# Eight cache buffers, packed query blocks, a new stream order and a PSUM copy for the last norm

## The chip, the cores and the metric

The kernel runs on one core of a Trainium2 chip. Time is device microseconds (us) of one execution. A core has TensorE (PE in the rows, its weight loads PEld), VectorE (DVE), ScalarE (ACT), GpSimd (POOL) and SyncE (SP), which here only issues transfers. SBUF holds data and weights, PSUM is where matmuls land.

## The reference, cut to what matters

One step of a one-layer decoder over 256 prompt tokens and 8 sequences of 8 new tokens (T = 320 columns), in float32. Two attention branches read the same normed input: branch 0 picks blocks of 256 keys and takes a softmax, branch 1 is stick-breaking.

```
h = rms_norm(x, g_mix);  qa, ka, va, qs, ks, vs, ga, gs = split(h @ w_in)
o_a = moba_block(rope(qa), cached + new keys and values)      # 8 heads of 64
o_s = stick_breaking_block(qs, cached + new keys and values)  # 8 heads of 64
x  = x + (sigmoid(ga) * (o_a @ w_branch_moba) + sigmoid(gs) * (o_s @ w_branch_sb)) @ w_out
x  = x + (silu(h2 @ w_gate) * (h2 @ w_up)) @ w_down           # h2 = rms_norm(x, g_ffn)
y  = rms_norm(x, g_final)
```

The cache of each sequence is 8 pages of 128 rows, found by a page table; keys and values of both branches together are 64 tiles of 1 MiB.

## The kernel before, in words

Activations lie transposed, features on the 128 partitions and the 320 tokens in columns. A float32 weight tile of 512 KiB is loaded raw (`load_weights`, three raw buffers `wr`) and split into a high part `wh` (an ACT copy, L152) and a rest `wl` (a DVE subtraction, L153), in three pairs of buffers; each dense product is three matmuls of 320 columns (L185, L344), 24 for one tile of output. A raw buffer is free for the next load when its `wl` is written, and a pair when PE has used it.

The first part of the program, up to about half of the span, interleaves six streams. The string `ORDER` (L52) has one letter for each step, and `Plan.run` takes them in that order; the letters set the order on PE, POOL and SP, while DVE and ACT are ordered by a scheduler when the kernel is built. Names for steps in this text:

- **d**: dense work: d1 to d8 queries and keys of branch 0, d9 to d14 its values, d15 to d22 queries and keys of branch 1, then its values and the first branch projection; **g1** to **g16**: the gates.
- **s**: scores of new queries against cached keys (L571), for a pair of sequences in two halves: S1a, S1b, S2a, S2b, S3a and so on. Each half needs two key tiles.
- **a**: three steps for each pair: T1 transposes the weights of pair 1, V1a and V1b multiply them with cached values (L691), two value tiles each; then T2, V2a, V2b. **e**: the end of a pair. **p**: the prompt's own attention.

Cache tiles, keys and values alike, go through one ring of `RB` buffers (`craw`); a buffer is free when the step that reads its tile is done. After each step `Loads.feed` starts at most one cache tile and as many weight tiles as fit. `FIRST` gives the loads begun ahead of the steps: w a weight tile, c a cache tile. Weights and keys go through SP's queue, in program order: if one load has to wait for its buffer, all behind it wait. Values go through POOL's queue as indirect transfers (L541), each behind a copy of one element (L540, `seen`) of the key tile begun next to last, so a value load starts only when that key tile has landed.

The scores multiply a block of 32 query columns, which is PE's stationary side, with 512 key columns; the blocks stand in two tiles `QS` (L592). `rsqrt` (L250) forms the first norm from `sq`, a sum of squares, with six tiny matmuls `cs` (L261) that stand on PE between d3 and d4. At the end `last_norm` (L838) makes the row r in SBUF on DVE, and seven multiplications (L854) form the output, six of 320 columns on DVE and one of 640 on POOL; each is followed by its store, by turns from SP and ACT.

Of the kernel before, what the change touches and what calls it, by code (L numbers as in the profile page):

```python
# [6 lines left out]
F32 = mybir.dt.float32  # L7
F32R = mybir.dt.float32r
I32 = mybir.dt.int32
AF = mybir.ActivationFunctionType  # L10
ALU = mybir.AluOpType
# [3 lines left out]
P = 128  # L15
# [16 lines left out]
SCALE = 0.125  # L32

SB, TB, OB, DB = 2, 3, 1, 2
RB = 7

LAG = 2
PACE = 1
FIRST = "wcwwwcwc"
ORDERED = {mybir.EngineType.PE, mybir.EngineType.Pool, mybir.EngineType.SP}  # L40
STARTED = ORDERED | {mybir.EngineType.DVE, mybir.EngineType.Activation}
WR, WB = 3, 3
# [7 lines left out]


ORDER = (  # L52
    "dddddddsddddsddsaddpsaadasegdsdaaapeddsadpsggdaappeaapdddssp"
    "gpepdgddpsagasapggegapaapgpsseggpggpdsagdasaaedgaaded"
)


# [82 lines left out]
class Net:  # L140
# [60 lines left out]
    def constants2(self):  # L201
        nc, I, c = self.nc, self.I, self.cpool
        self.ident = c.tile([P, P], F32, name="ident")
        self.ones = c.tile([P, P], F32, name="ones")
        self.warm = c.tile([P, 1], F32, name="warm")
        self.seen = c.tile([1, 1], F32, name="seen")
        self.keys = []
        turn = self.fpool.tile([P, HP, T], F32, name="turn", tag="F5", bufs=FB)
        self.cosr, self.sinr = turn[:, 0], turn[:, 1]
        self.rstd = c.tile([P, T], F32, name="rstd")  # L210
        self.rtok = c.tile([P, 3], F32, name="rtok")
        self.diag = c.tile([P, P], F32, name="diag")
        self.small = c.tile([P, NSMALL + NINT], F32, name="small")
        self.g_mix, self.g_ffn, self.g_fin = (self.small[:, 8 * i:8 * i + 8] for i in range(3))
        self.own_mask = [self.small[:, 24 + OWN * i:24 + OWN * (i + 1)] for i in range(2)]
        self.order = self.small[:, 24 + 2 * OWN:24 + 2 * OWN + 4]
        self.eps = self.small[:, 24 + 2 * OWN + 4:24 + 2 * OWN + 5]
        ints = self.small[:, NSMALL:].bitcast(I32)
        nk = DEC_B * N_PAGES
        self.pidx = ints[:, 0:2]  # L220
        self.idx_k = ints[:, 2:2 + nk]
        self.idx_v = ints[:, 2 + nk:].rearrange("p (h b) -> p h b", h=2)
        nc.vector.memset(self.ones, 1.0)

        self.keep_warm(WARM)

    def keep_warm(self, n):

        warm = self.pp.tile([P, 512], F32, name=self.uid("warm"), tag="t", bufs=TB)
        for _ in range(n):  # L230
            self.nc.tensor.matmul(warm, self.ones, self.ones[:, 0:1].to_broadcast([P, 512]), start=True, stop=True)

    def constants3(self):
        nc, I = self.nc, self.I
# [311 lines left out]
    def gen_scores(self, br, u, box):  # L546

        nc, w = self.nc, self.work
        for half in range(2):
            yield (f"qk{br}{int(br or half)}3",), f"s{br}{u}" if half else None  # L550
            raw = [self.loads.take("c") for x in range(2)]
            if half == 0:
                QS = self.made.pop((br, u), None) or self.queries(br, u)
                box["S"] = []
                p = box["p"] = w.tile([P, 8, N_PAGES, 16], F32, name=self.uid("p"), tag="p", bufs=1)
                if br == 0:
                    st = box["st"] = w.tile([P, 32], F32, name=self.uid("st"), tag="st", bufs=2)
                else:
                    s = box["s"] = w.tile([P, NCOL], F32, name=self.uid("s"), tag="s0", bufs=1)
                    kp = box["kp"] = w.tile([P, NCOL + 1], F32, name=self.uid("kp"), tag="s2", bufs=1)  # L560

                    zo = self.own_scores(br, u, QS)
                    nc.vector.memset(kp[:, 0:1], 1.0)
                    nc.scalar.activation(kp[:, 1:1 + OWN], zo, AF.Sigmoid, scale=-SCALE)
                    nc.scalar.activation(s[:, :OWN], zo, AF.Sigmoid, scale=SCALE)
            S = self.pp.tile([P, 512], F32, name=self.uid("S"), tag="s", bufs=SB)
            box["S"].append(S)
            for i in range(2):
                for y in range(4):
                    x, hp, r = y // 2, 2 * (y % 2) + i, slice(32 * y, 32 * y + 32)  # L570
                    nc.tensor.matmul(S[r], QS[:, hp, r], raw[x][:, :, hp * P:(hp + 1) * P], start=i == 0, stop=i == 1)  # L571
            if br == 0:
                Sb = S.rearrange("p (b k) -> p b k", b=2)
                nc.vector.tensor_reduce(st[:, 2 * half:2 * half + 2], Sb, AX.X, ALU.add)
                nc.vector.tensor_reduce(st[:, 15 + 2 * half:17 + 2 * half], Sb, AX.X, ALU.max)
            else:
                c0, c1 = OWN + 512 * half, OWN + 512 * (half + 1)
                nc.scalar.activation(kp[:, c0 + 1:c1 + 1], S, AF.Sigmoid, scale=-SCALE)
                nc.scalar.activation(s[:, c0:c1], S, AF.Sigmoid, scale=SCALE)
                f0 = c0 if half else 0  # L580
                n = c1 - f0 - half
                nc.vector.tensor_tensor_scan(kp[:, f0 + 1:f0 + 1 + n], kp[:, f0 + 1:f0 + 1 + n], self.zeros.to_broadcast([P, n]),
                                             initial=kp[:, f0:f0 + 1], op0=ALU.mult, op1=ALU.add)
                a, d = (v[:, c0:c1].rearrange("p (g j q) -> p j g q", g=4, j=8) for v in (s, kp))
                nc.vector.tensor_mul(p[:, :, 4 * half:4 * half + 4], a, d)
        if br == 0:
            box["zo"] = self.own_scores(br, u, QS)
        later = divmod(HP * br + u + 2, HP)
        if later[0] == br or f"qk{later[0]}03" in self.plan.done:
            self.queries(*later)  # L590

    def queries(self, br, u):  # L592

        nc, t, QS = self.nc, self.B[br], self.QS[u % 2]
        qbase = QS.rearrange("p a b -> p (a b)")
        for e in range(2):
            r = slice(HD * e, HD * e + HD)
            src = t["q"][r, :, NP_ + 16 * u:NP_ + 16 * u + 16].rearrange("p h (x q) -> p h x q", x=2)
            c = qbase[r, 8 * e:8 * e + 8]
            dst = bass.AP(tensor=c.tensor, offset=c.offset, ap=[list(c.ap[0]), [P + 16, HP], [64, 2], [1, 8]])  # L600
            if e:
                nc.scalar.activation(dst, src, AF.Copy)
            else:
                nc.vector.tensor_copy(dst, src)
        self.made[br, u] = QS
        return QS

    def own_scores(self, br, u, QS):
        nc = self.nc
        own = self.pp.tile([P, 512], F32, name=self.uid("own"), tag="t", bufs=TB)  # L610
        for i in range(2):
            for y in range(4):
                x, hp, r = y // 2, 2 * (y % 2) + i, slice(32 * y, 32 * y + 32)
                c = NP_ + 16 * u + 8 * x
                nc.tensor.matmul(own[r, :OWN], QS[:, hp, r], self.B[br]["k"][:, hp, c:c + OWN], start=i == 0, stop=i == 1)
        zo = self.work.tile([P, OWN], F32, name=self.uid("zo"), tag="zo", bufs=2)
        nc.vector.tensor_tensor(zo, own[:, :OWN], self.own_mask[br], ALU.add)
        return zo
# [219 lines left out]
    def last_norm(self, acc, xg):  # L838

        nc, y, x1 = self.nc, self.stg, self.x1  # L840
        ps = self.pp.tile([P, T], F32, name="rb", tag="o", bufs=OB)
        nc.tensor.matmul(ps, self.ones, acc[:, 0], start=True, stop=False)
        for c in (slice(0, T // 2), slice(T // 2, T)):
            nc.tensor.matmul(ps[:, c], self.ones, acc[:, 1, c], start=False, stop=c.stop == T)
        r, w = [y.tile([P, T], F32, name=n, tag="y", bufs=3) for n in ("r", "w")]
        nc.scalar.activation(r, ps, AF.Abs_reciprocal_sqrt, scale=1.0 / D)
        nc.vector.tensor_mul(w, r, r)
        nc.vector.scalar_tensor_tensor(w, w, -0.5 / D, ps, op0=ALU.mult, op1=ALU.mult)
        nc.vector.scalar_tensor_tensor(r, w, 1.5, r, op0=ALU.add, op1=ALU.mult)
        e = 0  # L850
        for i, n in enumerate((1, 1, 1, 1, 1, 1, 2)):
            s = slice(e, e + n)
            engine = nc.gpsimd if i == 6 else nc.vector
            engine.tensor_tensor(x1[:, s], xg[:, s], r[:, None, :].to_broadcast([P, n, T]), ALU.mult)  # L854
            (nc.scalar if i % 2 else nc.sync).dma_start(self.O["y"][:, s], x1[:, s])
            e += n

# [23 lines left out]
    def build(self):  # L881
# [38 lines left out]
        with ExitStack() as top:  # L920
# [8 lines left out]
            with ExitStack() as mid:  # L929
# [7 lines left out]
                self.constants3()  # L937
                self.loads.begin(FIRST[2:])
                self.work = mid.enter_context(pool("work"))
                self.QS = [self.work.tile([P, HP, P], F32, name=f"QS{i}") for i in range(2)]  # L940
                self.zeros = self.work.tile([P, 1], F32, name="zeros")
                for t in (*self.QS, self.zeros):
                    nc.vector.memset(t, 0.0)
# [99 lines left out]
```

## Time and profile before

| | |
|---|---|
| median of 3 runs | 565.85 us (564.5 to 568.01) |
| profiled execution, its own time | 564.84 us |
| its span, first to last instruction | 563.0 us |
| mean granted clock of TensorE | 0.986 of full speed |
| PE, DVE, ACT, POOL busy | 96%, 59%, 48%, 9% |
| read from HBM | 134.22 MB |

How to read the rows below. A row of a timeline has its start in the span, its length, the engine, the line, output and inputs, the count, and in brackets how long the engine stood idle before it and what ended that. The chain of waits is followed back from the last instruction. PE's matmuls overlap each other: a matmul of 320 columns is listed with 0.31 us, but 24 of them follow each other in 3.52 us, so lengths of work are taken from groups in the chain. A window gives the busy time of each engine in a stretch, the granted clock, the share of the 16 DMA engines and the rate in GB/s.

### The profile page before, as it was taken

What the parts mean: (1) busy time and instruction counts of PE and PEld (TensorE: products, weight loads), DVE (VectorE), ACT (ScalarE), POOL (GpSimd) and SP (SyncE); (2) the same over time, 40 slices, a digit from 0 to 9 for tenths busy, and PEclk for the clock granted to TensorE, in tenths of its full rate; (3) what the DMA queues carried; (4) which work ended last, traced back from release to release, by engine and by line L of the source; (5) the groups of instructions that cost most, each with busy time, mean ns of one, the idle gap of its engine ahead of it and who ended that gap; (6) DMA issues with size and microseconds to landing.
All of it is one profiled execution on the core that took longest, in us unless ns stands there. A gap on an engine that the chain in (4) does not pass through costs nothing.

```text
span 563.0 us, 10934 instructions
## 1 busy us (share of the span) xinstructions
PE 543.2 (96%) x4252; PEld 494.0 (88%) x4252; DVE 332.7 (59%) x600; ACT 268.7 (48%) x483; POOL 48.8 (9%) x73
## 2 busy tenths in 40 slices
PE   8899999799999999999999999999999999999992
PEld 6888867578778787977999999999999999999992
DVE  6777675255575746764688656666666665444434
ACT  7775555325675444643446454444444443354321
POOL 0002102140021402131000000000000000000001
PEclk9899999799999999999999999999999999999997
DMA  8899999999699999987595544444444444544512
GB/s 306 296 374 331 368 358 405 413 392 400 225 363 357 352 401 351 383 316 293 198 325 162 150 130 151 146 150 154 149 146 152 150 152 140 153 141 144 161 33 93
DMA packets 45571, 138.86 MB, mean 247 GB/s; under 512 B 5200, under 2 KB 7504, under 8 KB 41296
## 3 DMA queue, kind: packets, MB, share of 16 engines
q1 hardware_dynamic: 40336, 104.06, 54.4%
q0 software_dynamic: 4608, 33.56, 15.0%
q8 instruction: 33, 0.54, 0.4%
q10 hardware_dynamic: 576, 0.56, 0.3%
q14 instruction: 18, 0.15, 0.1%
HBM read 134.22 MB, written 3.93 MB: 245 GB/s over the span
## 4 chain that ended last, share of the span: by engine, by line
PE 81%; DMA 7%; ACT 5%; DVE 3%; SPq 2%; issue 1%; DVEq 0%; POOL 0%; ACTq 0%
PE dps L185 55%; PE dps L344 12%; PE S L571 4%; PE po L691 4%; DMA vr<-in_cv,small 3%; DMA wr<-in_w_in 2%; ACT rot L363 2%; DMA kr<-in_ck 1%; PE dps L388 1%; PE tp L667 1%; PE dps L518 1%; PE tp L504 1%; ACT wh L152 1%; PE dps L463 1%; DVE wl L153 1%
## 5 line engine op out<-in xcount | busy, mean ns | idle before, releaser
L152 ACT ACTIVATE wh<-wr 128x1024 fp32r<-128x1024 f32 (+1 forms) x122 | 127.0, 1045 | 187.0 <-issue 110.9
L153 DVE TENSOR_TENSOR wl<-wr,wh 128x1024 fp32r<-128x1024 f32 (+1 forms) x122 | 146.8, 1205 | 76.9 <-ACT wh L152 76.7
L185 PE MATMUL dps<-x1h,wh 128*128 128x320 f32 x352 | 109.0, 310 | 0.0
L185 PE MATMUL dps<-x1l,wh 128*128 128x320 f32 x352 | 108.8, 309 | 0.0
L185 PE MATMUL dps<-x1h,wl 128*128 128x320 f32 x352 | 108.8, 309 | 0.0
L344 PE MATMUL dps<-xs,wh 128*128 128x320 f32 x256 | 78.5, 319 | 1.6 <-ACT wh L152 1.4
L344 PE MATMUL dps<-xl,wh 128*128 128x320 f32 x256 | 77.2, 314 | 0.2 <-DVE xl L307 0.2
L185 PEld LDWEIGHTS dps<-x1h,wh 128*128 128x128 f32 x352 | 66.1, 188 | 0.1
L185 PEld LDWEIGHTS dps<-x1l,wh 128*128 128x128 f32 x352 | 66.1, 188 | 0.0
L185 PEld LDWEIGHTS dps<-x1h,wl 128*128 128x128 f32 x352 | 66.1, 188 | 0.0
L185 PE MATMUL dps<-fh,wl 128*128 128x320 f32 x176 | 54.4, 309 | 0.0
L185 PE MATMUL dps<-fh,wh 128*128 128x320 f32 x176 | 54.4, 309 | 0.0
L185 PE MATMUL dps<-fl,wh 128*128 128x320 f32 x176 | 54.4, 309 | 0.0
L344 PEld LDWEIGHTS dps<-xs,wh 128*128 128x128 f32 x256 | 48.7, 190 | 4.7 <-ACT wh L152 1.5
L344 PEld LDWEIGHTS dps<-xl,wh 128*128 128x128 f32 x256 | 48.8, 191 | 0.9 <-DVE xl L307 0.9
L344 PE MATMUL dps<-xs,wl 128*128 128x320 f32 x256 | 43.6, 310 | 0.0
L344 PEld LDWEIGHTS dps<-xs,wl 128*128 128x128 f32 x256 | 39.3, 189 | 0.3 <-DVE wl L312 0.3
L541 POOL DMA_INDIRECT vr<-in_cv,small x32 | 33.3, 1040 | 43.1 <-PE po L691 11.4
L691 PE MATMUL po<-vr,pt 128*32 128x256 f32 x512 | 32.3, 394 | 4.4 <-DMA vr<-in_cv,small 4.4
L185 PEld LDWEIGHTS dps<-fh,wh 128*128 128x128 f32 x176 | 33.0, 188 | 0.0
L185 PEld LDWEIGHTS dps<-fl,wh 128*128 128x128 f32 x176 | 33.0, 188 | 0.0
L185 PEld LDWEIGHTS dps<-fh,wl 128*128 128x128 f32 x176 | 33.0, 188 | 0.0
(203 smaller groups left out, 848.9 us busy)
## 6 DMA issues: line engine op xcount, KB each, us to landing
kr<-in_ck SPq DMA_DIRECT2D x128, 256.0 KB
wr<-in_w_ff SPq DMA_DIRECT2D x44, 512.0 KB
wr<-in_w_in SPq DMA_DIRECT2D x30, 512.0 KB
wr<-in_w_down SPq DMA_DIRECT2D x16, 448.0 KB
wr<-in_w_v SPq DMA_DIRECT2D x8, 512.0 KB
wr<-in_w_b SPq DMA_DIRECT2D x8, 512.0 KB
wr<-in_w_out SPq DMA_DIRECT2D x8, 512.0 KB
wr<-in_w_down SPq DMA_DIRECT2D x8, 512.0 KB
```

The lines of the kernel that those rows point to most:

```text
L152: self.nc.scalar.activation(hi, raw, AF.Copy)
L153: self.nc.vector.tensor_tensor(lo, raw, r32(hi), ALU.subtract)
L185: nc.tensor.matmul(ps, w, x, start=first and i == 0, stop=last and i == len(todo) - 1)
L344: self.nc.tensor.matmul(ps, a, x, start=k + low + i == 0, stop=low == 1 and k + n == KD and i == n - 1)
L363: nc.scalar.activation(rot[32 * q:32 * q + 32], ps[32 * s:32 * s + 32], AF.Copy)
L388: nc.tensor.matmul(ps, self.xs[:, k], w[k][j], start=k + j == 0, stop=k + j == KD)
L463: nc.tensor.matmul(S[e][:, i], q[r, 2 * u + i, half * P:half * P + P], k[r, 2 * u + i, half * P:NP_], start=True, stop=True)
L504: nc.tensor.transpose(tp[:, i * P:(i + 1) * P], src, self.ident)
L518: nc.tensor.matmul(po[r, i, :NP_ if kt else P], t["v"][:, kt, c0:c0 + HD], mv, start=kt == 1, stop=kt == 0)
L541: self.nc.gpsimd.indirect_dma_start(out=raw.rearrange("p a b -> p (a b)"), out_offset=None, in_=self.I[f"cv{br}"], in_offset=bass.Indirect ...
L571: nc.tensor.matmul(S[r], QS[:, hp, r], raw[x][:, :, hp * P:(hp + 1) * P], start=i == 0, stop=i == 1)
L691: nc.tensor.matmul(po[r], PT[j][:, r], v[:, c:c + 256], start=j == 0, stop=j == 8)
```

## The change

- `RB` goes from 7 to 8 cache buffers (8 KiB more of each partition). Room comes from `QS`, two tiles of 320 columns in place of 512 (blocks of 32 columns that overlap where they hold zeros), and from `ones`, one column in place of 128, which matmuls now read broadcast.
- `FIRST` goes from "wcwwwcwc" to "wwwwc": two cache tiles and one weight tile fewer are begun ahead of the steps, and the fourth weight tile comes ahead of the first key tile.
- `ORDER` is new from its 12th letter to its 61st.
- In `last_norm` ACT copies r into a PSUM bank; five of DVE's six output multiplications read that copy.

```diff
-RB = 7
+RB = 8
-FIRST = "wcwwwcwc"
+FIRST = "wwwwc"
-    "dddddddsddddsddsaddpsaadasegdsdaaapeddsadpsggdaappeaapdddssp"
+    "dddddddsdddsdddsdaspaddsadasegaddaapedsapdpsggdaapepaaddgpds"
...
-        self.ones = c.tile([P, P], F32, name="ones")
+        self.ones = c.tile([P, 1], F32, name="ones")
...
-                    nc.tensor.matmul(S[r], QS[:, hp, r], raw[x][:, :, hp * P:(hp + 1) * P], start=i == 0, stop=i == 1)
+                    nc.tensor.matmul(S[r], self.block(QS, x, hp), raw[x][:, :, hp * P:(hp + 1) * P], start=i == 0, stop=i == 1)
...
-            dst = bass.AP(tensor=c.tensor, offset=c.offset, ap=[list(c.ap[0]), [P + 16, HP], [64, 2], [1, 8]])
+            dst = bass.AP(tensor=c.tensor, offset=c.offset, ap=[list(c.ap[0]), [48, HP], [160, 2], [1, 8]])
...
+    def block(self, QS, x, hp):
+
+        c = 48 * hp - 16 * (hp % 2)
+        return QS[:, x, c:c + 32]
...
+        ones = self.ones.to_broadcast([P, P])
+        nc.tensor.matmul(ps, ones, acc[:, 0], start=True, stop=False)
...
+        rb = self.pp.tile([P, T], F32, name="rstd3", tag="s", bufs=SB)
+        nc.scalar.activation(rb, r, AF.Copy)
...
-            engine = nc.gpsimd if i == 6 else nc.vector
-            engine.tensor_tensor(x1[:, s], xg[:, s], r[:, None, :].to_broadcast([P, n, T]), ALU.mult)
+            engine, v = (nc.gpsimd, r) if i == 6 else (nc.vector, rb if i else r)
+            engine.tensor_tensor(x1[:, s], xg[:, s], v[:, None, :].to_broadcast([P, n, T]), ALU.mult)
...
-                self.QS = [self.work.tile([P, HP, P], F32, name=f"QS{i}") for i in range(2)]
+                self.QS = [self.work.tile([P, 2, 160], F32, name=f"QS{i}") for i in range(2)]
```

Three places show what the change moves. The first is DVE near the start, around d3 (`wl_164` and `wl_152` are the rest of d3's weights, `wl_259` that of d4's, `sq` is what `cs` reads):

```order
-L153 TENSOR_TENSOR wl_164<-wr_122,wh_163 128x1024
+L153 TENSOR_TENSOR wl_152<-wr_122,wh_151 128x1024
 L319 TENSOR_TENSOR sq_106<-sq_106 128x1280
+L153 TENSOR_TENSOR wl_259<-wr_124,wh_258 128x1024
 L319 TENSOR_TENSOR sq_106<-sq_106 128x640
 L321 TENSOR_TENSOR sq<-sq_106 128x320
```

The weights of d4 are now split between the first and the last two additions of `sq`. Before, they were split behind them, as ACT copied their high part only behind eight copies `rot`; on ACT that copy has moved ahead of the eight.

The second place is SP's queue where the keys of S3a (`kr_889` before, `kr_768` now) are begun. Before:

```order
L157 DMA wr_656<-in_w_in 128x1024
L157 DMA wr_692<-in_w_in 128x1024
L157 DMA wr_694<-in_w_in 128x1024
L157 DMA wr_825<-in_w_in 128x1024
L157 DMA wr_827<-in_w_in 128x1024
L529 TENSOR_LOAD small
L533 ISA
L533 DMA kr_889<-in_ck 128x512
```

and now:

```order
L157 DMA wr_601<-in_w_in 128x1024
L157 DMA wr_659<-in_w_in 128x1024
L157 DMA wr_695<-in_w_in 128x1024
L157 DMA wr_697<-in_w_in 128x1024
L529 TENSOR_LOAD small
L533 ISA
L533 DMA kr_768<-in_ck 128x512
```

The weights of d18 and d19 (`wr_825`, `wr_827`) stood ahead of these keys and now stand behind them; what stands ahead are those of d15, d16, d17 and g1. On PE, V2a and V2b stood together behind d18; now V2a stands ahead of d18, and V2b behind d19.

The third place is the end of DVE's program; the seventh row of the multiplications is POOL's and unchanged:

```order
-L849 SCALAR_TENSOR_TENSOR r<-w,r 128x320
-L854 TENSOR_TENSOR x_3741<-xg,r 128x320 x6
...
+L855 SCALAR_TENSOR_TENSOR r<-w,r 128x320
+L863 TENSOR_TENSOR x_3741<-xg,r 128x320
+L863 TENSOR_TENSOR x_3741<-xg,rstd_6371 128x320 x5
```

Five of the six now read `rstd`, the copy in PSUM, which ACT writes behind r.

## Rows read from the trace of the kernel before

**Rows 1.** The page: granted TensorE clock in 40 equal slices, in tenths

```profile
PEclk9899999799999999999999999999999999999997
```

**Rows 2.** Who PE waited for: us in total, times, longest

```profile
PE po L691 <- DMA vr<-in_cv,small: 4.4, 2, 3.5
PE dps L344 <- ACT wh L152: 1.4, 1, 1.4
...
PE S L571 <- ACT QS L602: 0.9, 1, 0.9
...
PE dps L185 <- DVE wl L153: 0.5, 1, 0.5
```

**Rows 3.** The chain that ended last, in order of time: start, us, what

```profile
50.72 1.89 PE dps L388 x16
...
66.58 1.23 DVE wl L153
...
88.11 14.16 DMA vr<-in_cv,small
102.31 4.44 PE po L691 x36
...
171.59 3.52 PE dps L344 x24
...
191.03 2.16 PE po L691 x40
...
329.70 221.98 PE dps L185 x1512
...
557.64 1.61 DVE x L854 x4
```

**Rows 4.** Windows: busy time of PE, PEld, DVE, ACT, POOL, then clock, DMA share, GB/s

```profile
0.00:60.00 60.00, 55.47 (x368) 47.84 (x369) 40.98 (x85) 42.16 (x83) 5.21 (x15) 0.97 0.93 332
60.00:90.00 30.00, 30.00 (x284) 22.91 (x286) 19.00 (x48) 16.91 (x44) 6.28 (x9) 1.00 0.97 359
90.00:105.00 15.00, 10.60 (x120) 6.51 (x116) 6.17 (x18) 5.62 (x16) 2.29 (x4) 0.83 1.03 419
...
20.00:25.00 5.00, 4.52 (x20) 4.52 (x21) 4.02 (x8) 2.79 (x5) 0.00 (x0) 0.66 0.59 197
...
100.00:105.00 5.00, 2.69 (x28) 1.31 (x32) 0.00 (x0) 0.00 (x0) 1.88 (x3) 0.50 1.06 420
```

**Rows 5.** Timelines of ACT, DVE and PE near the start, and PE at V2a

```profile
15.84 3.51 ACT L363 ACTIVATE rot<-dps 32x320 f32<-32x320 f32 x8
...
31.55 1.06 ACT L152 ACTIVATE wh<-wr 128x1024 fp32r<-128x1024 f32 x1 [2.95 <-DMA wr<-in_w_in]
...
17.72 0.49 DVE L321 TENSOR_TENSOR sq<-sq 128x320 f32<-128x320 f32 x1
...
18.27 0.83 PE L261 MATMUL cs<-ones,sq 128*128 128x1 f32 x6 [0.29 <-DVE sq L321]
...
95.36 1.93 PE L691 MATMUL po<-vr,pt 128*32 128x256 f32 x32
```

**Rows 6.** Timeline of SP's queue at the keys of S3a; value tiles, issue to landing

```profile
50.63 17.53 SPq L157 DMA_DIRECT2D wr<-in_w_in  x5
69.33 1.93 SPq L533 DMA_DIRECT2D kr<-in_ck  x4
...
DMA to landing us min/median/max: 6.3/9.7/14.2
```

**Rows 7.** Timelines of DVE and POOL: two instructions that overlap

```profile
237.14 0.49 DVE L438 TENSOR_TENSOR y<-dps,rstd 128x320 f32<-128x320 f32 x1 [0.98 <-PE dps L344]
...
237.34 0.18 POOL L540 COPY seen<-kr 1x1 f32<-1x1 f32 x1
```

**Rows 8.** The output multiplications L854: duration in ns min/median/max; POOL's row

```profile
L854 DVE TENSOR_TENSOR x<-xg,r x6: 478/480/1817, 555.4 to 558.8; 128x320 f32<-128x320 f32 x6
...
555.70 1.60 POOL L854 TENSOR_TENSOR x<-xg,r 128x640 f32<-128x640 f32 x1 [299.98 <-DVE r L849]
```

More of the change, by code (lines that the diff above doesn't have):

```diff
@@ L52 @@
 ORDER = (
-    "dddddddsddddsddsaddpsaadasegdsdaaapeddsadpsggdaappeaapdddssp"
-    "gpepdgddpsagasapggegapaapgpsseggpggpdsagdasaaedgaaded"
+    "dddddddsdddsdddsdaspaddsadasegaddaapedsapdpsggdaapepaaddgpds"
+    "spepdgddpsagasapggegapaapgpsseggpggpdsagdasaaedgaaded"
 )
@@ L230, in keep_warm @@
         for _ in range(n):
-            self.nc.tensor.matmul(warm, self.ones, self.ones[:, 0:1].to_broadcast([P, 512]), start=True, stop=True)
+            self.nc.tensor.matmul(warm, self.ones.to_broadcast([P, P]), self.ones.to_broadcast([P, 512]), start=True, stop=True)
     def constants3(self):
@@ L614, in own_scores @@
                 c = NP_ + 16 * u + 8 * x
-                nc.tensor.matmul(own[r, :OWN], QS[:, hp, r], self.B[br]["k"][:, hp, c:c + OWN], start=i == 0, stop=i == 1)
+                nc.tensor.matmul(own[r, :OWN], self.block(QS, x, hp), self.B[br]["k"][:, hp, c:c + OWN], start=i == 0, stop=i == 1)
         zo = self.work.tile([P, OWN], F32, name=self.uid("zo"), tag="zo", bufs=2)
@@ L841, in last_norm @@
         ps = self.pp.tile([P, T], F32, name="rb", tag="o", bufs=OB)
-        nc.tensor.matmul(ps, self.ones, acc[:, 0], start=True, stop=False)
+        ones = self.ones.to_broadcast([P, P])
+        nc.tensor.matmul(ps, ones, acc[:, 0], start=True, stop=False)
         for c in (slice(0, T // 2), slice(T // 2, T)):
-            nc.tensor.matmul(ps[:, c], self.ones, acc[:, 1, c], start=False, stop=c.stop == T)
+            nc.tensor.matmul(ps[:, c], ones, acc[:, 1, c], start=False, stop=c.stop == T)
         r, w = [y.tile([P, T], F32, name=n, tag="y", bufs=3) for n in ("r", "w")]
```

## The prediction

> **What bounds the kernel now.** I read the granted clock first, then PE's waits, then the chain, then windows of the stretches where something waits. From 272 us on the chain is PE alone, one stretch of 222 us among it [rows 3]. The change leaves that work and its order as they are, so it can move the time in three places only: the start, the six streams up to 272 us, and the end behind the last matmul. Up to 272 us PE waits little: 4.4 us in two waits of V2b for its second pair of value tiles, and 1.4, 0.9 and 0.5 us near the start [rows 2]. To these come stretches at half clock (1.2 in place of 2.4 GHz), which show as slices below 9 [rows 1]: the windows 20 to 25 and 100 to 105 us have 0.66 and 0.50 [rows 4]. Both follow a gap on PE.
>
> What made V2b wait is a transfer. Its last value tile was begun at 88.11 and took 14.16 us [rows 3], the longest of the value tiles, whose median is 9.7 [rows 6]. In 90 to 105 us the DMA engines moved 419 GB/s at a share of 1.03, so they were full; in 60 to 90 us it was 359 GB/s, and in 0 to 60 us 332 [rows 4]. So the tile was late because less was moved earlier, not for want of engines at the end. One reason stands in SP's queue: five weight loads took it from 50.63 for 17.53 us, since each waits until a raw buffer has been split, and the keys of S3a behind them began only at 69.33 [rows 6].
>
> **Term 1, the wait of V2b.** It costs 4.4 us of idle [rows 2] and a slow stretch: 36 matmuls took 4.44 us where 40 take 2.16, that is 1.94 for 36, so 2.50 more [rows 3]. Together 6.9 us.
>
> Three edits meet here. The order puts V2a ahead of d18 and V2b behind d19. A dense step is 3.52 us [rows 3], so V2a, at 95.36 [rows 5], comes 3.5 earlier and V2b as much later; with the 0.9 us of term 2, V2a starts at about 90.9. The weights of d18 and d19 no longer hold up the keys of S3a. The last of the four weight loads still ahead of them waits for a split that follows the end of d11. That ends at 50.72 + 1.89 = 52.61 before [rows 3], now about 1 us later, since S1b, about 2 us by the value steps' row, goes ahead of it and 0.9 us are gained. The ACT copy (1.06, [rows 5]) and the DVE rest (1.23, [rows 3]) bring it to 56. So these keys begin at 56 to 58 in place of 69.33. And the eighth buffer lets each cache tile begin one tile earlier where buffers were what it waited for.
>
> What V2a needs by 90.9 is, in the order of the loads, 18 cache tiles of 1.05 MB, 20 weight tiles of 0.52 MB and 1.8 MB of inputs and constants: 31.2 MB, and with some 1 MB of later tiles that share the engines 32.2. By 60 us 332 x 60 = 19.9 MB were there [rows 4]; I take the same for after: its queue starts poorer, with two cache tiles fewer begun, but the hole at 20 to 25 us, 197 GB/s [rows 4], closes, as the raw buffer of d4's weights is split sooner. The other 12.3 MB take 29.4 us at 419 GB/s and 34.3 at 359 [rows 4]. So they are there between 89.4 and 94.3. I take the rate between, 389: 91.6, a wait of 0.7. V2b then has two dense steps, 7 us, more for its two tiles, and I expect no wait there. For what I cannot see I make the rest 1.2 us: a gain of 6.9 - 1.2 = 5.7. The bounds are 6.9, and 0.5 where the rate stays at 359: then V2a waits 3.4 to 3.9 and the slow stretch comes too, 6.4 in all.
>
> **Term 2, the start.** Between d3 and d4 PE waits for `cs` 0.29 us, runs it from 18.27 [rows 5], and waits 1.4 for d4's weights [rows 2], because ACT made eight `rot` copies first, 3.51 us from 15.84 [rows 5]. Now the weights' copy goes ahead of the eight, so d4 needn't wait. But on DVE their rest, 1.23 us [rows 3], goes ahead of the last additions of `sq`, which ended at 18.21 [rows 5]; so `cs` comes 1.2 us later, and the wait only moves: a gain of 0.2. The gap stays about as long, so I leave the slow stretch behind it. It would give back some 1.7 us: the clock missing in the window 20 to 25, 0.34 x 5 us [rows 4]. Later S1a waits 0.9 for the query blocks, which ACT copies behind three groups of `rot`, and d9 0.5 for weights [rows 2]. ACT had stood 2.95 us for the weight tile ahead of these groups [rows 5]; with no key tile in front of it that tile comes sooner, but one more weight copy of 1.06 us now stands ahead of the query blocks. I take half of the 1.4: 0.7. Term 2 is 0.9, between -1.1 (the copy has no cover) and 3.3.
>
> **Term 3, the end.** Of DVE's six multiplications five take 0.48 us and one 1.82, while POOL's runs 1.60 from 555.70 [rows 8]: with both inputs in SBUF the second DVE row ended only behind POOL's. A DVE row with one input in PSUM overlapped a POOL copy at 237.3, and neither was longer than alone [rows 7]. So five rows that read the copy should run through POOL's. DVE's first row, 0.48 from 555.41, covers ACT's copy of r, which by 1.06 us for 1024 columns [rows 5] I put at 0.5 with its hand-over, so the second begins at about 556.0. Rows follow each other every 0.40 (four in 1.61, [rows 3]), so the sixth ends at 558.1 in place of 557.64 + 1.61 = 559.25: 1.15 us. If a long POOL row does block it, unlike the short copy, the gain is 0, and the hand-over makes it -0.5.
>
> **Term 4, what costs.** Steps have new neighbours: S2b comes close behind S2a, the two halves of the prompt's second pair stand almost together, d18 and d19 follow V2a. PE's waits of this kind now are 0.3 to 0.9 us [rows 2, 5]. I charge one, 0.3, between 0 and 1.5. At nothing I cost `ones` as one column and the query blocks: as many instructions of the same size on PE; the fill of the blocks on DVE shrinks and lies ahead of nothing that PE waits for.
>
> **Sum.** 5.7 + 0.9 + 1.15 - 0.3 = 7.45 us. The profiled execution's own time of 564.84 becomes 557.4. It lies 1.0 below the median of the runs, 565.85, from which I take the same: 558.4, 1.3% less.
>
> **Rivals.** The first, the transfers stay the bound: the eighth buffer doesn't raise the rate, because SP stood on splits of weights and not on cache buffers [rows 6]. Then V2a waits as V2b did, term 1 is 0.5, the sum 2.25, and the time 563.6. For it speaks a share of 0.93 and 0.97 already [rows 4]; against it 419 GB/s behind 359, and that the keys of S3a leave the jam. The Trainium skill has a rule for it (DMA: Bandwidth & Descriptors, "Where 436 GB/s comes from"): between HBM and SBUF the memory's side binds at about 358 GB/s for a core. By it the rate of 60 to 90 us was the ceiling and the time would be this rival's 563.6. The 419 GB/s over 15 us differ from it, so I give this rival no more than its other reasons earn.
>
> The second, the start's slow stretch goes with its cause: if `cs` comes less late than I think, PE stays at full clock, and 1.7 us more are gained: 556.7. Against it: the moved wait is as long as the old.
>
> The third, slower. The value tiles of V1b are now held by `seen` until the keys of S3a have landed, where before an earlier key tile sufficed. PE reaches V1b at about 78: from there to V2a, 90.9, stand V1b itself with 2.2 us, d17 with 3.5, T2 with 1, S3b with 2, and e1 and g1 with 3.7 [rows 3]. If these keys still began at 69.33, as before [rows 6], I put their landing 4 us behind their last issue, at 75; the second value tile, 1.3 later, lands 9.7 to 14.2 after that [rows 6], at 86 to 90, a wait of 8 to 12 us with a slow stretch of 2.5. That alone is some 12.5; the tiles of V2 come late by as much and the 5.7 of term 1 are lost: 565.85 + 12.5 - 1.75 = 576.6. It decides from keys that begin later than 62 (78 less 9.7, 1.3 and 5). I have them at 56.
>
> **How the numbers follow.** The forecast gets 0.60, the first rival 0.24, the second 0.10, the third 0.06. About 1% (5.7 us) is what a measurement can tell from no change: faster means under 560.2. The forecast falls beyond that with 0.07 of its 0.60 (a wait of 3 us or more at V2a), and all but a sixth of the second rival lies under it: faster 0.61; the first rival and the 0.07 make same 0.33; slower 0.06. The range takes in the first rival and goes down to where terms 1 to 3 are near their best (6.9 + 3.3 + 1.3 = 11.5): 554.5 to 564.5.
>
> **What would show it.** Term 1: PE's waits for value tiles in 60 to 110 us under 2 us in sum, no clock below 0.9 there, the rate of 60 to 90 us above 380 GB/s, the keys of S3a begun by 60. Term 2: `cs` starts at about 19.5 and d4 right behind it. Term 3: no multiplication over 0.6 us on DVE. Wrong would be a wait as long as the old at V2a or V1b, a new wait of PE behind 110 us where the same bytes are now wanted some 7 us earlier, or a row of 1.8 us at the end.

## The result and the profile after

The changed kernel takes 559.05 us (median of 4 runs, 557.76 to 559.79) beside 566.31 us for the kernel before (median of 4): ratio 0.987, interval 0.9833 to 0.9907. Run again beside the experiments it took 558.35 us, ratio 0.9865 (0.9843 to 0.9886). The forecast was 558.4 us and faster by over 1%: both hold. The sum behind it holds less well, as its terms show.

The granted clock of the profiled execution (span 558.0 us), to be read against [rows 1], then who PE waited for, against [rows 2] (us in total, times, longest):

```profile
PEclk9899999999999999999999999999999999999998
```

```profile
PE po L696 <- DMA vr<-in_cv,small: 2.9, 3, 1.3
PE cs L261 <- DVE sq L321: 1.3, 1, 1.3
```

The low slice at 98 to 112 us (the 7) is gone, the one at 14 to 28 us is there. The wait for value tiles (L691 is L696 now) is 2.9 us in place of 4.4, and no piece is longer than 1.3. Windows of the same stretches as [rows 4] (busy PE, PEld, DVE, ACT, POOL, then clock, DMA share, GB/s):

```profile
0.00:60.00 60.00, 56.40 (x382) 47.94 (x386) 40.75 (x87) 43.85 (x87) 3.67 (x12) 0.97 0.94 343
60.00:90.00 30.00, 29.38 (x292) 21.46 (x285) 19.66 (x50) 13.07 (x33) 7.81 (x12) 1.00 0.99 364
90.00:105.00 15.00, 13.67 (x134) 11.02 (x132) 6.34 (x16) 7.99 (x19) 2.29 (x4) 1.00 1.02 413
20.00:25.00 5.00, 4.70 (x23) 4.70 (x24) 3.78 (x13) 3.51 (x6) 0.00 (x0) 0.66 1.04 361
100.00:105.00 5.00, 5.00 (x61) 3.96 (x59) 2.88 (x5) 1.31 (x2) 0.00 (x0) 1.00 1.03 415
```

The rates are a little higher up to 90 us (343 and 364 for 332 and 359), and there is no half clock at 100 us. PE at the two value steps that still wait, V1b (from 77.86) and V2a (from 91.91):

```profile
77.86 0.60 PE L696 MATMUL po<-vr,pt 128*32 128x256 f32 x4
79.08 1.71 PE L696 MATMUL po<-vr,pt 128*32 128x256 f32 x26 [0.62 <-DMA vr<-in_cv,small]
...
91.91 0.63 PE L696 MATMUL po<-vr,pt 128*32 128x256 f32 x4
93.86 1.92 PE L696 MATMUL po<-vr,pt 128*32 128x256 f32 x28 [1.33 <-DMA vr<-in_cv,small]
```

SP's queue around the keys of S3a (the eight `kr`), and POOL's around V1b's two value tiles:

```profile
46.22 10.73 SPq L157 DMA_DIRECT2D wr<-in_w_in  x4
58.12 5.04 SPq L533 DMA_DIRECT2D kr<-in_ck  x8
```

```profile
64.90 0.18 POOL L540 COPY seen<-kr 1x1 f32<-1x1 f32 x1 [13.24 <-DMA kr<-in_ck]
65.73 1.90 POOL L541 DMA_INDIRECT vr<-in_cv,small  x1 [0.65 <-DMA kr<-in_ck]
67.64 0.18 POOL L540 COPY seen<-kr 1x1 f32<-1x1 f32 x1
67.98 0.97 POOL L541 DMA_INDIRECT vr<-in_cv,small  x1 [0.16 <-issue]
```

The keys begin at 58.12 in place of 69.33 [rows 6]. But `seen` holds V1b's value tiles until 64.90; the second begins at 67.98 and PE goes on at 79.08, 11.1 us later, where it had been ready before. V2a's two value tiles are held in the same way, until 81.18, and the second is begun at 83.23:

```profile
81.18 0.18 POOL L540 COPY seen<-kr 1x1 f32<-1x1 f32 x1 [12.24 <-DMA kr<-in_ck]
...
83.23 0.97 POOL L541 DMA_INDIRECT vr<-in_cv,small  x1 [0.16 <-issue]
```

The end of the program, DVE and then POOL:

```profile
551.38 0.49 DVE L863 TENSOR_TENSOR x<-xg,r 128x320 f32<-128x320 f32 x1
551.86 2.08 DVE L863 TENSOR_TENSOR x<-xg,rstd 128x320 f32<-128x320 f32 x5
```

```profile
551.66 1.60 POOL L863 TENSOR_TENSOR x<-xg,r 128x640 f32<-128x640 f32 x1 [302.18 <-DVE r L855]
```

The five rows that read the copy in PSUM run through POOL's row in 2.08 us; none stalls as the one of 1.82 did [rows 8].

**Where the time went, by places of equal work.** Between fixed points of PE's program the lengths mostly repeat to 0.1 us from run to run wherever PE doesn't wait, so a stretch that is longer has a wait or a slow clock in it. The points are the starts of S2a, of S4a and of the last stretch of 1512 matmuls (329.70 before, [rows 3]), and the end of the span. S2a and S4a before, then S2a, S4a and the last stretch in the changed kernel:

```profile
60.37 1.92 PE L571 MATMUL S<-kr,QS 128*32 128x512 f32 x16
115.87 1.92 PE L571 MATMUL S<-kr,QS 128*32 128x512 f32 x16
```

```profile
59.06 1.92 PE L571 MATMUL S<-kr,QS 128*32 128x512 f32 x16
110.91 1.49 PE L571 MATMUL S<-kr,QS 128*32 128x512 f32 x12
325.67 221.97 PE dps L185 x1512
```

Medians belong to the runs, the other columns to one profiled execution each. The profile of the row "changed, again" is called the second profile below; the rows under it are the experiments of the next section.

| kernel | to S2a | S2a to S4a | to last stretch | to the end | median us | ratio to before, interval |
|---|---|---|---|---|---|---|
| before | 60.37 | 55.50 | 213.83 | 233.30 | 566.31 | |
| changed | 59.06 | 51.85 | 214.76 | 232.33 | 559.05 | 0.987 (0.9833 to 0.9907) |
| changed, again | 57.94 | 51.34 | 215.07 | 232.35 | 558.35 | 0.9865 (0.9843 to 0.9886) |
| e1_seven | 59.08 | 53.05 | 218.84 | 232.33 | 563.84 | 0.9943 (0.9909 to 0.9977) |
| e2_oldstream | 66.42 | 56.70 | 213.97 | 232.31 | 568.41 | 1.0041 (1.0024 to 1.0059) |
| e5_firstold | 64.54 | 48.65 | 214.30 | 232.31 | 561.09 | 0.9902 (0.9867 to 0.9936) |
| e13_oldorder | 58.10 | 55.57 | 214.47 | 232.36 | 561.66 | 0.9902 (0.987 to 0.9934) |
| e10_packonly | 62.10 | 56.03 | 214.48 | 233.59 | 570.34 | 1.0083 (1.0049 to 1.0118) |
| e7_gate | 58.38 | 49.83 | 213.32 | 232.37 | 555.5 | 0.981 (0.9785 to 0.9835) |
| e7_again | 58.30 | 50.49 | 214.21 | 232.30 | 557.34 | 0.9848 (0.9809 to 0.9888) |
| e9_gate2 | 57.98 | 51.30 | 213.73 | 232.39 | 557.59 | 0.9861 (0.9841 to 0.9882) |
| e12_gate1 | 57.54 | 53.32 | 215.93 | 232.31 | 560.27 | 0.9892 (0.9849 to 0.9935) |
| e3_oldtail | 57.88 | 51.53 | 214.76 | 233.63 | 558.91 | 0.9882 (0.9858 to 0.9905) |
| e4_tailsbuf | 58.81 | 51.55 | 214.63 | 233.61 | 559.47 | 0.9881 (0.9855 to 0.9908) |

The experiments ran in three groups, each on one chip with the kernel before beside them (medians 565.94, 565.97 and 566.64 us); the first group is e1, e2, e5 and e7_gate, the second the changed kernel again, e3, e4 and e9, the third the rest. Four rows (changed, changed again, e3, e4) are kernels that differ by their edits at the end alone. Among them the first column scatters by 1.2 us, the second by 0.5 and the third by 0.4, so smaller differences in a column mean nothing by themselves.

### The profile page after: what moved, and what is told of

Same layout as the page of the kernel before. It is cut to its first block, busy times and chain, and to the rows that moved or that the text cites. A ratio compares the mean times of both kernels' runs of the same rounds, so it can differ in the third digit from the quotient of the medians.

```text
span 558.0 us, 10927 instructions
## 1 busy us (share of the span) xinstructions
PE 542.0 (97%) x4252; PEld 493.2 (88%) x4252; DVE 329.7 (59%) x600; ACT 269.9 (48%) x484; POOL 49.8 (9%) x73
## 4 chain that ended last, share of the span: by engine, by line
PE 82%; DMA 9%; DVE 3%; ACT 2%; SPq 1%; issue 1%; POOL 1%; DVEq 0%; POOLq 0%; ACTq 0%
PE dps L185 55%; PE dps L344 15%; PE po L696 4%; DMA vr<-in_cv,small 4%; DMA kr<-in_ck 3%; PE S L571 3%; DMA wr<-in_w_in 1%; DVE wl L153 1%; SPq L533 1%; PE tp L504 1%; PE tp L672 1%; PE dps L518 1%; PE dps L388 1%; PE dps L463 1%; DMA small<-in_c_small 1%
## 5 line engine op out<-in xcount | busy, mean ns | idle before, releaser
L541 POOL DMA_INDIRECT vr<-in_cv,small x32 | 35.9, 1121 | 19.1 <-PE po L696 8.6
L696 PE MATMUL po<-vr,pt 128*32 128x256 f32 x512 | 32.1, 381 | 2.9 <-DMA vr<-in_cv,small 2.9
```

The source lines that it names most:

```text
L541: self.nc.gpsimd.indirect_dma_start(out=raw.rearrange("p a b -> p (a b)"), out_offset=None, in_=self.I[f"cv{br}"], in_offset=bass.Indirect ...
L696: nc.tensor.matmul(po[r], PT[j][:, r], v[:, c:c + 256], start=j == 0, stop=j == 8)
```

## The experiments

### The parts apart: buffers, order, first loads, packing

The question: which part brings the gain in the middle, S2a to S4a. Each edit is against the changed kernel.

**e1_seven**: one buffer less.

```diff
-RB = 8
+RB = 7
```

> The changed kernel with seven cache buffers in place of eight; all else is as changed. Theory (the order did it: V2b stands a dense step later, the keys of S3a no longer wait behind the weights of d18 and d19): value waits of PE in 60 to 110 us stay under 4 us in sum, no clock below 0.9 there, about 560 to 561 us, some 1 to 2 above the changed kernel. Rival (the eighth buffer did it): the long wait comes back at V1b, V2a or V2b, 4 us or more with a stretch at half clock, 564 to 566 us.

It took 563.84 us, with single runs from 559.48 to 568.46. That is close to the rival's time, but not by the rival's wait: V1b, V2a and V2b wait for no tile, and no half clock follows. The start is as in the changed kernel; the middle is 1.2 to 1.7 us longer, and behind S4a 3.8 to 4.1 more are lost, where the next value step, V3a, waits 2.96 us. In the middle S3a, begun at 76.14, waits for a key tile:

```profile
80.52 1.48 PE L571 MATMUL S<-kr,QS 128*32 128x512 f32 x10 [3.33 <-DMA kr<-in_ck]
```

```profile
60.00:90.00 30.00, 26.67 (x254) 19.55 (x250) 17.01 (x41) 12.87 (x32) 6.89 (x12) 1.00 0.91 338
```

The rate of 60 to 90 us is 338 GB/s where eight buffers have 364 and, in the second profile, 373: the eighth buffer does raise it, and with this order it is worth 4 to 5.5 us, most of it later than the prediction looked.

**e2_oldstream**: eight buffers, packing and the new end, with the order and first loads of before.

```diff
-FIRST = "wwwwc"
+FIRST = "wcwwwcwc"
-    "dddddddsdddsdddsdaspaddsadasegaddaapedsapdpsggdaapepaaddgpds"
-    "spepdgddpsagasapggegapaapgpsseggpggpdsagdasaaedgaaded"
+    "dddddddsddddsddsaddpsaadasegdsdaaapeddsadpsggdaappeaapdddssp"
+    "gpepdgddpsagasapggegapaapgpsseggpggpdsagdasaaedgaaded"
```

> Eight buffers, packed query blocks and the PSUM copy at the end, but ORDER and FIRST of before. Theory (the order did it): V2b still waits about 4 us and the clock falls behind it; what is left of the gain is the end, 1.3 us, and little more: 564 to 565 us. Rival (the eighth buffer did it): the wait at V2b is under 1.5 us, no half clock there, 559 to 561 us.

It is slower than before, 568.41, and both expectations missed. I read its SP queue first, where six weight loads stood for 24.95 us ahead of S3a's keys, and took the old order for the cause. The table says otherwise: against the kernel before, 6.05 us are lost ahead of S2a and 1.2 in the middle (this profiled execution is 2.8 us over its kernel's median). Most of the loss at the start is a wait for weights with a slow stretch behind it:

```profile
48.22 0.38 PE L185 MATMUL dps<-wh,xs 128*128 128x256 f32 x1 [1.56 <-ACT wh L152]
49.48 0.58 PE L185 MATMUL dps<-wl,xs 128*128 128x256 f32 x1 [0.88 <-DVE wl L153]
49.86 0.41 PE L185 MATMUL dps<-wh,xl 128*128 128x256 f32 x1
50.08 0.41 PE L185 MATMUL dps<-wh,xs 128*128 128x256 f32 x1
```

Rows of 0.28 us at full clock are 0.41 here, and they follow each other every 0.21 us in place of 0.12; the granted clock of 50 to 55 us is 0.50.

**e5_firstold**: the old first loads alone, **e13_oldorder**: the old order alone; each takes its one edit from the diff of e2.

> The changed kernel with FIRST of before (wcwwwcwc): the first key tile goes into the queue ahead of the fourth weight tile. Theory (bytes bound V1b and V2a): the DMA share of 10 to 15 us goes from 0.43 to about 1.0, so 1 MB more is moved early, the waits at V1b and V2a (1.9 us as listed) shrink by 1 to 2 us; at the start the 1.3 us wait ahead of cs turns back into a wait of 1.4 us ahead of d4: 557 to 558.5 us. Rival (these waits come from the gate and from the queue's order): they stay within 0.5 us, time within 1 us of the changed kernel.

> The changed kernel with the order of the kernel before, but the new first loads (in the run e2_oldstream both were old: 568.4). It parts the two. Theory: the old order is what hurts, since five to six weight loads stand ahead of S3a's keys, and the first loads only cost at the start: 565 to 567, keys of S3a not begun before 68, a value wait of 3 us or more. Rival: the old first loads made that jam, since two more cache tiles taken at the start leave the queue poorer; then 560 to 562.

Between e13 and e2 only the first loads differ: 58.10 against 66.42 us up to S2a. So the time that I had expected of e13 was wrong and its rival's was right: 561.66. The jam in SP's queue is there all the same, as is a wait of V2b for a value tile, so in the middle nothing is gained:

```profile
46.68 19.41 SPq L157 DMA_DIRECT2D wr<-in_w_in  x5
67.26 4.96 SPq L533 DMA_DIRECT2D kr<-in_ck  x8
```

```profile
100.59 3.20 PE L696 MATMUL po<-vr,pt 128*32 128x256 f32 x26 [3.50 <-DMA vr<-in_cv,small]
```

Between e13 and the changed kernel only the order differs: 55.57 against 51.85 and 51.34. This is what the new order brings with eight buffers, 3.7 to 4.2 us. e5 took 561.09 us, above both expectations: the waits at V1b and V2a went, as its theory said, but the start lost more than they gave. It comes to S2a 5.5 to 6.6 us later, and then waits for no value tile between S2a and S4a, 48.65 us. A late PE gives the transfers time; so about half of what is lost at the start comes back.

**e10_packonly**: the kernel before with the packed query blocks and the one column of ones, and nothing else of the change.

```diff
-        self.ones = c.tile([P, P], F32, name="ones")
+        self.ones = c.tile([P, 1], F32, name="ones")
...
-                    nc.tensor.matmul(S[r], QS[:, hp, r], raw[x][:, :, hp * P:(hp + 1) * P], start=i == 0, stop=i == 1)
+                    nc.tensor.matmul(S[r], self.block(QS, x, hp), raw[x][:, :, hp * P:(hp + 1) * P], start=i == 0, stop=i == 1)
```

> The kernel before with the packed query blocks and ones as one column alone: seven buffers, the old order, the old first loads and the old end. The prediction costed these two edits at nothing. Theory: the time of the kernel before within 1 us, 565 to 567, and its wait at V2b. Rival: a smaller stationary tile that lies closer together, or ones read with a step of zero, costs or gives back something on each of these matmuls; then the time differs by more than 1.5 us and the score steps (1.74 us from S to V) are longer or shorter.

It is 3.7 us slower than the kernel before beside it (570.34 for 566.64), so "at nothing" was wrong, and not by way of the matmuls that read the blocks: S2b to V1a is 1.9 us in both (69.8 to 71.7 and 71.6 to 73.5). DVE and ACT are ordered by the scheduler when the kernel is built, and here it made another order; which of the two edits led it there, the smaller fills or the column of ones, no run tells. ACT's instructions between the queries of S1 and the first values, before and then e10 (`wh_583` and `wh_649` are weights, `rot_641` reads what PE makes in the step ahead):

```
L152 ACTIVATE wh_544<-wr_367 128x1024
L152 ACTIVATE wh_583<-wr_456 128x1024
L363 ACTIVATE rot_641<-dps_616 32x320 x4
L383 ACTIVATE v_234<-dps_658,rtok 128x256
L152 ACTIVATE wh_649<-wr_509 128x1024
```

```
L152 ACTIVATE wh_544<-wr_367 128x1024
L363 ACTIVATE rot_641<-dps_616 32x320 x4
L152 ACTIVATE wh_583<-wr_456 128x1024
L152 ACTIVATE wh_649<-wr_509 128x1024
L383 ACTIVATE v_234<-dps_658,rtok 128x256
```

In the trace of e10 the `rot` waits for PE, the copy of `wh_583` behind it ends at 46.73, and PE, which needs it, stands:

```profile
41.63 1.06 ACT L152 ACTIVATE wh<-wr 128x1024 fp32r<-128x1024 f32 x1
43.89 1.75 ACT L363 ACTIVATE rot<-dps 32x320 f32<-32x320 f32 x4 [1.20 <-PE dps L344]
45.67 1.06 ACT L152 ACTIVATE wh<-wr 128x1024 fp32r<-128x1024 f32 x1
```

```profile
46.78 0.39 PE L185 MATMUL dps<-wh,xs 128*128 128x256 f32 x1 [0.87 <-ACT wh L152]
48.04 0.39 PE L185 MATMUL dps<-wl,xs 128*128 128x256 f32 x1 [0.87 <-DVE wl L153]
```

In this execution, the quickest of the seven of e10, the span is 3.2 us longer than before's; 2.0 of them lie between S1a and S2a, where these waits are (24.13 us for 22.09), and the granted clock stays at 1.00 behind them; in e2 it falls to 0.50 from 50 to 55 us behind 1.56 and 0.88 us. The other runs of e10 have a lower mean clock (0.976 to 0.990 for 0.991), so a slow stretch may make up the rest of the 3.7; no trace of theirs shows where.

The same two waits stand in e2 and e5, the other kernels with packed blocks and the old first loads, and in no kernel with the new ones. With the packing the new first loads are worth 6.7 us in the old order (e2 to e13, medians on two chips) and 2.0 to 2.7 in the new one (e5 to the changed kernel). What they are worth without the packing is not known, since no run has them alone. In the trace of before, which has neither, this cost and its cure can't be seen.

### What held V1b

The question: is it the gate `seen` that delays V1b, or are the engines too full to bring its tiles sooner. Three kernels change which key tile holds the value loads.

**e7_gate**, V1b's two loads wait for the fourth last key tile:

```diff
-            self.nc.gpsimd.tensor_copy(self.seen, self.keys[-LAG][0:1, 3, 511:512])
+            back = 4 if (br, b // 2, half) == (0, 0, 1) else LAG
+            self.nc.gpsimd.tensor_copy(self.seen, self.keys[-back][0:1, 3, 511:512])
```

> The changed kernel, where the two value tiles of V1b follow an older key tile (the fourth from last begun, as before the change) in place of the keys of S3a. Theory (the gate makes V1b wait): they are begun some 3 us sooner, at about 61 to 63 in place of 65.7 and 68.0, and V1b does not wait; 1 to 1.5 us less than the changed kernel. Rival (the engines are full, so what V1b gains V2a or S3a loses): the wait at V1b goes, that at V2a grows by as much, time within 0.5 us.

> The kernel of e7_gate once more, on another chip. Theory: 555.5 again, no loss at V1b, and none at the value step at 184 us. Rival: that run was lucky in when single transfers landed, as the scatter of the changed kernel's waits suggests; then 557 to 559.

**e12_gate1**, the same with `back = 1`: the last key tile.

> The changed kernel with the two value loads of V1b held until the last key tile in the queue has landed, instead of the one before it: the opposite of e7_gate. Theory (the gate sets V1b): these loads begin some 2 to 3 us later, at 66 to 68 us, V1b loses 3 to 4.5 us instead of 1.0 to 1.3, the streams behind it come later by as much, and the time is 561 to 562. Rival (the loads would wait for full engines anyway, and e7_gate won by chance): 558 to 559.

**e9_gate2**, as e7_gate, with V2a's two loads (`(0, 1, 0)`) among those that wait for the fourth last.

> The changed kernel with the two value loads of V1b and the two of V2a held by the landing of the fourth last key tile instead of the second last (in the run e7_gate it was V1b's alone, 555.5). Theory (the gate, not the engines, set when value tiles came): V2a's tiles begin at about 70 instead of 79 to 81, its wait of 0.55 goes, and the time is 0.5 to 1 us under that run, about 554.8. Rival (the engines are full by then): the bytes of V2a's tiles delay the keys of S3b or the weights of d17 and d18, PE waits there by 1 to 3 us, and the time is 556 to 558.

V1b of e7_gate, its second tile begun at 61.88 (POOL, then PE):

```profile
60.58 0.96 POOL L542 DMA_INDIRECT vr<-in_cv,small  x1 [9.57 <-DMA kr<-in_ck]
61.55 0.18 POOL L541 COPY seen<-kr 1x1 f32<-1x1 f32 x1
61.88 0.96 POOL L542 DMA_INDIRECT vr<-in_cv,small  x1 [0.16 <-issue]
```

```profile
77.15 1.91 PE L697 MATMUL po<-vr,pt 128*32 128x256 f32 x32
78.88 0.61 PE L697 MATMUL po<-vs,pto 128*32 128x256 f32 x8
79.42 0.41 PE L344 MATMUL dps<-xs,wh 128*128 128x320 f32 x1
```

And V1b of e12_gate1, where the second tile began at 69.01:

```profile
76.32 0.60 PE L697 MATMUL po<-vr,pt 128*32 128x256 f32 x4
79.42 3.20 PE L697 MATMUL po<-vr,pt 128*32 128x256 f32 x26 [2.50 <-DMA vr<-in_cv,small]
```

From the start of V1b to the next dense matmul it is 2.27 us with the tile begun at 61.88 (e7_gate), 3.50 with 67.98 (changed), and 6.93 with 69.01 (e12_gate1, with a slow stretch behind the wait). That V1b follows the gate is shown. What it is worth in the end is less than that: in e12_gate1 V2a no longer waits, so the middle is only 1.5 to 2.0 us longer than in the changed kernel, and the time, 560.27, lies between what theory and rival gave.

e7_gate is the fastest kernel of this study, 555.5 us on one chip and 557.34 on another, against 559.05 and 558.35 of the changed kernel on two chips. Both profiles lose nothing at V1b, and nothing at the value step at 184 us, as the theories said. But the second run's time is the rival's 557 to 559 and not 555.5 again, and the intervals of the two kernels touch, so I put the gain at 1 to 3.5 us and no closer.

e9_gate2 gained nothing more: 557.59, the rival's time. V2a's loads begin at 68.12 and 69.43 us and V2a waits no more, but S3b does: SP's issue of its keys takes 13.76 us in place of 8.46 in e7_gate, and they come late. V2a, then SP and S3b:

```profile
92.22 1.93 PE L697 MATMUL po<-vr,pt 128*32 128x256 f32 x32
```

```profile
67.54 13.76 SPq L533 DMA_DIRECT2D kr<-in_ck  x8
```

```profile
86.39 1.48 PE L572 MATMUL S<-kr,QS 128*32 128x512 f32 x10 [0.77 <-DMA kr<-in_ck]
```

So a gate can shift the wait from one step to another. That it paid at V1b and not at V2a fits with V1b's tiles being needed ahead of S3b's keys and V2a's behind them; these two pairs of tiles are all that was tried.

### The end

**e3_oldtail**: no copy, all rows read r. **e4_tailsbuf**: the copy in SBUF instead of a bank.

```diff
-        rb = self.pp.tile([P, T], F32, name="rstd3", tag="s", bufs=SB)
+        rb = y.tile([P, T], F32, name="rstd3", tag="y", bufs=3)
```

> The changed kernel with the end of the kernel before: all six multiplications read r in SBUF, no copy in a bank. Theory: one DVE row takes about 1.8 us again, and DVE ends 1.1 to 1.3 us later behind the last matmul; time 560.2, 1.2 us over the changed kernel. Rival: the long row was covered by the stores that still land behind it, since the first five rows' stores queue on the same engines; then DVE ends later and the time is the same within 0.4 us.

> The changed kernel, but ACT writes its copy of r into a tile in SBUF instead of a PSUM bank, and the five DVE rows read that. It tells apart what frees DVE: Theory (place of the input): with both inputs in SBUF again one DVE row waits for POOL's row of 1.6 us and takes about 1.8 us, as with the old end, and the time is the old end's or 0.1 more. Rival (sharing of one tile): DVE and POOL got in each other's way by reading the same tile r; then a second copy anywhere suffices, no row is over 0.6 us, and the time is the changed kernel's.

> The changed kernel once more, on the same chip as the runs beside it, so that they are compared with it and not only with the kernel before. Expected: 559 us, ratio 0.987 to the kernel before. If a wait of V1b or V2a depends on when single transfers land, it should show again with another size (0.5 to 2 us); the slow stretch near 20 us may be there or not.

DVE's rows of e3, then those of e4 behind the same first row, and of e4's five the durations in ns (min/median/max):

```profile
549.88 3.84 DVE L861 TENSOR_TENSOR x<-xg,r 128x320 f32<-128x320 f32 x6
```

```profile
550.69 0.49 DVE L863 TENSOR_TENSOR x<-xg,r 128x320 f32<-128x320 f32 x1
551.25 3.27 DVE L863 TENSOR_TENSOR x<-xg,rstd 128x320 f32<-128x320 f32 x5
```

```profile
L863 DVE TENSOR_TENSOR x<-xg,rstd x5: 477/478/1667, 551.2 to 554.0; 128x320 f32<-128x320 f32 x5
```

Six rows in 3.84 us, and five in 3.27, one of them 1.67, where the bank gives 2.08: a second copy is no help, its place is. From the start of the last stretch to the end it is 233.63 and 233.61 us against 232.35 in the changed kernel beside them, so the copy in PSUM is worth 1.3 us. The medians (558.91 and 559.47 for 558.35) are of that sign, with overlapping intervals, and e3's is 0.6 us over the changed kernel where 1.2 was expected. The changed kernel itself lost 0.9 us at V1b and 1.4 at V2a in the second profile, other sizes than the 1.2 and 1.95 of the first, and had no slow stretch near 20 us. The Trainium skill (SBUF — State Buffer, "Who interferes with whom") gives the reason, a port pair that DVE and GpSimd share under an exclusive lock; the rows agree, since only inputs that both lie in SBUF stall beside POOL's 1.60 us.

## Why the prediction was right, and where its steps were not

**Term 1, the wait of V2b: right in kind, too large.** The old wait and its slow stretch are gone, V2b takes 2.30 us and waits for nothing. But the middle gained 3.65 us (55.50 to 51.85; 4.16 in the second profile), not 5.7. The step that failed is "I make the rest 1.2 us". The rest is 3.2 and 2.7, read against the 48.65 us of e5 in which nothing waits: V1b's 1.2 and 0.9, V2a's 1.95 and 1.4, and in the second profile 0.3 at S3b. The listed waits in 60 to 110 us, 0.62 and 1.33, stay just under the 2 us that the prediction asked for; they are less than what the steps lost.

**The rate: two errors that cancelled.** I kept 19.9 MB by 60 us and took 389 GB/s for 60 to 90. Measured are 343 x 60 = 20.6 MB and 364 GB/s, so "above 380" failed. By these V2a's 32.2 MB are there at 91.7 us (10.9 MB more by 90, and the last 0.7 MB at 413 GB/s in 1.7 us), the 91.6 of the forecast. But PE came to V2a at 91.91 and went on at 93.86: the last tile, held by `seen`, was begun only at 83.23 and landed 10.6 us later. In e9_gate2 these tiles are begun at 68.12 and 69.43, and V2a waits for nothing. So at V2a it was not the count of bytes that decided but the hold by `seen`, which the prediction weighed for V1b alone.

**The third rival was there, small.** It was V1b held by `seen`, and it was to decide from keys begun later than 62. They began at 58.12 and V1b still lost 1.2 us. The bound was mis-sized in its parts: `seen` opened 6.8 us behind the first issue of the keys where I had 5, the second value tile followed 3.1 us behind the first gate where I had 1.3, and took 11.1. By these 21.0 us the keys would have had to begin at 57.

**Term 2, the start: too small.** 0.9 was forecast, 1.3 and 2.4 us were gained by S2a (2.5 and 1.6 in e3 and e4, with the same start). `cs` came at 20.30 and 19.05 in place of 19.5, with d4 right behind it as said. From d4 to S1a it is 16.8 us (20.99 to 37.78) for 17.8 before, and from S1a to S2a 21.3 for 22.1: in the first profile the waits for the query blocks and for d9's weights went, more than the half that I took. The second rival's price was wrong too: in the second profile the granted clock of 20 to 25 us was 1.00, not 0.66, and d4 to S1a took 16.7 us all the same. PE then stood 0.82 us ahead of `rb` (L275, which spreads the norm's row) and 0.33 us for the query blocks from ACT, so what the full clock gave there was waited away.

**Term 3, the end: right.** 1.15 was forecast; DVE ends 1.3 us sooner behind the last stretch. Of this 0.97 arrives at the end of the span, against the one profile of before. The other 0.3 us lie behind the last row of DVE; the copy didn't cost them, since e3 and e10, which have the old end, show them too (233.63 and 233.59 for 233.30). What did is open.

**Term 4, new waits: in its bounds.** 0.3 forecast, 0.9 and 1.2 measured behind S4a. One value step at 185 us alone costs 1.6 and 1.3 us by equal work against e7_gate. It is a new wait behind 110 us, which the prediction named as a sign of being wrong:

```profile
186.85 1.71 PE L696 MATMUL po<-vr,pt 128*32 128x256 f32 x26 [0.96 <-DMA vr<-in_cv,small]
```

It is absent from e7_gate, e7_again and e9_gate2, where the step's two tiles are begun at 169 to 173 us in place of 173 to 178, and longest in e12_gate1 (1.56 us listed). Why a gate at 65 us still shows there is open.

**What was costed at nothing** cost 3.7 us by itself (e10), part of it through ACT's order as traced, and with the new first loads the two waits are gone. The prediction saw neither, and the sum did not show it because both are in the change.

**The first rival**, that the transfers stay the bound, was half right. They still set the middle: the changed kernel's remaining waits there are all for tiles, and in e9_gate2 letting V2a's tiles through made S3b wait for its keys. But the eighth buffer does raise the rate (338 to 364), against what the rival said. The Trainium skill's ceiling of 358 GB/s (DMA: Bandwidth & Descriptors, "Where 436 GB/s comes from") does not show here either: 413 GB/s for 15 us.

By the profiled pair the terms are 1.3 + 3.65 - 0.9 + 0.97 = 5.0 us (563.0 to 558.0), with the second profile 6.3; the medians moved 7.3 and 7.6. That the forecast's 7.45 was near the medians is in part luck. In the second profile term 1 was too large by what term 2 was too small, 1.5 us each. In the first pair they don't cancel (2.05 and 0.4); there the profile before was 1.5 us under its median and the profile after 0.7 over.

## What to carry to other kernels

Divide the program into stretches of equal work at fixed points of the engine that never idles: the lengths repeat to about 0.1 us where nothing waits, so most of what is lost has an address, and a run that waits nowhere gives the floor. Where a scheduler orders some engines, print those engines' order too when an edit seems free, since packing moved a weight copy here, and the kernel with it alone lost more than most of the waits that the change was about. When transfers are the bound, an earlier start of one tile can make another late: e7_gate gained by it, e9_gate2 did not.

## What the runs showed of the hardware that I had not expected

PE's listed wait is too short at a value step. The weight loads of the same steps in the changed kernel:

```profile
79.08 1.22 PEld L696 LDWEIGHTS po<-vr,pt 128*32 128x32 f32 x26 [1.10 <-DMA vr<-in_cv,small]
93.86 1.44 PEld L696 LDWEIGHTS po<-vr,pt 128*32 128x32 f32 x28 [1.81 <-DMA vr<-in_cv,small]
```

PE's rows say 0.62 and 1.33 us, the weight loads 1.10 and 1.81, and the steps are 1.2 and 1.95 us longer than where nothing waits (2.27 in e7_gate, 1.86 in e9_gate2). The row of the weight load is the closer one to cost a wait from. And behind a wait of 2.5 us on PE stood a slow stretch (e12_gate1: 26 matmuls in 3.20 us for 1.71, granted clock 0.74 from 80 to 85 us), while behind the waits of 0.6 and 1.3 us stood none. The length of the wait alone doesn't decide it: behind the 3.33 us of S3a in e1 the clock stayed at 1.00 from 75 to 85 us, and behind the 2.96 us of V3a at 1.00 from 115 to 120.
